# Gating each expert's result as it is stored, and summing the stored rows and the residual ahead of the last products

## The chip, the cores and the metric

The kernel runs on one core of one Trainium2 chip. The metric is the device time of one execution in microseconds; times are given as the median of several runs. TensorE is called PE here, its weight loads PEld, VectorE DVE, ScalarE ACT, GpSimd POOL, and SyncE, which issues most of the DMAs, SP.

## The reference

The program is a trunk of two layers over 256 context rows and 256 latent rows of width 1024. Each layer first mixes tokens and then runs a mixture of 32 experts, of which every row uses two. The change lies in the first layer's mixture, where all 512 rows take part. Cut to what matters:

```
h_c = layer_norm(xc) * (1 + cscale2) + cshift2
h_l = layer_norm(x)  * (1 + scale2)  + shift2
ffn = moe(concat([h_c, h_l]))          # each row: sum over its 2 experts of
                                       #   w[row, e] * swiglu(row; gate[e], up[e]) @ down[e]
xc = post_norm(ALPHA * xc + cgate2 * ffn[:256])
x  = post_norm(ALPHA * x  + gate2  * ffn[256:])
```

The gate is one row of 1024 numbers for all context rows (`cgate2`) and another for all latent rows (`gate2`). These are the two classes of tokens. `post_norm` is a layer norm with a scale and an offset.

## The kernel before

The 512 rows lie in four tiles of 128: tiles 0 and 1 are context, tiles 2 and 3 latent. An expert takes up to 64 rows. For each expert of the first mixture `expert0` (L1769) gathers its rows from DRAM with an indirect DMA on POOL, multiplies them with the gate and up weights (`product`, L1722, four loads of 1 MB), makes the activation `th` on ACT and DVE (`swiglu`, L1692), and multiplies with the down weights (`down`, L1733, two loads of 1 MB). Row `p` of the result has the first half of the columns of a slot in partitions 0 to 63 and the second half in 64 to 127. ACT copies it out of PSUM times the slot's weight `w` (L1787), and POOL scatters it to `yb_d` in DRAM with a second indirect DMA: rows 0 to 511 are the rows' first experts, rows 512 to 1023 their second. Two spare slots (32 and 33) take the 65th row and later ones of busy experts, at most 64 each; what goes beyond is left to the overflow loop.

The results of experts 30 and 31 aren't scattered. They are kept as a rounded part `yh` and the rest `yl` (L1784, L1785), and selection products with `slt` (L1933) add them to the tiles. This is what the title calls the last products.

After expert 29 SP loads, for tiles 0 and 1, both stored rows and the residual, and for tiles 2 and 3 the first stored row (L1912 to L1922). The two stored rows of tiles 0 and 1 are summed (L1917), and for each tile DVE adds the last products (L1937). Then comes `overflow` (L1512), a loop whose count is read from memory and is zero here; all engines meet at it. Behind it, for each tile: the gate product, for tiles 2 and 3 the second stored row, and the residual (L1948 to L1960), on DVE and POOL, and then `normed_affine` (L1961), which takes statistics on DVE, a power on POOL and two further steps on DVE. The next layer starts with a second norm over the same tiles (`h_in`, L471), whose result `xh` PE transposes.

Buffers are tiles of stacked pools; a tile waits until whoever used its place is done. The order on each queue is laid out when the program is built, by a list scheduler that follows a model of time and takes what is ready by priority; `tc.high_priority` and `tc.issue_after` bend it. Each engine then works through its queue in order. SP's queue too is in order: a load that waits for its buffer holds all behind it.

The second mixture (`experts1`, L1845) is not touched by the change, apart from the shared overflow code, where it keeps what it does.

## Time and profile before

| what | us |
|---|---|
| median of 3 runs | 2546.49 (2543.59 to 2548.29) |
| the profiled execution | 2547.03 |
| its span, first to last instruction | 2545.2 |
| PE busy | 2204.2 (87%) |
| DVE busy | 1396.3 (55%) |
| ACT busy | 693.5 (27%) |
| POOL busy | 719.0 (28%) |
| bytes moved by DMA | 710.71 MB, mean 279 GB/s |

The busy shares are means over stages with different limits. What the change is worth has to be read from its own stage: the slices show where a stage begins, the windows which engine fills it, the waits who holds whom up, and the timeline in what order. The chain that ended last is cut at the second mixture's overflow loop and reaches back only 14 us, so it says nothing on the first mixture.

### The profile page before, as it was taken

The page shows a single profiled execution, that of the slowest core. Times are in us where ns is not written, and L with a number is a line of the kernel's source. Part 1 is how long each engine was busy: PE and PEld are TensorE (multiplying, and loading weights), DVE is VectorE, ACT ScalarE, POOL GpSimd, SP SyncE. Part 2 cuts the span into 40 slices and gives each one's busy share as a digit, 9 for nine tenths or more (in the row PEclk, how much of TensorE's full clock was granted, in tenths as well). Part 3 has the DMA queues.
Part 4 walks back from the last instruction along what each step waited for, and adds up shares of the span by engine and source line. Part 5 has one row for each costly group of instructions (what it writes and reads, how often), then busy time and mean ns, then how long its engine had stood idle before and what let it go on. Part 6 is the DMA issues. An engine that isn't in the chain of part 4 may idle for free. (4 is left out here: it accounts for less than half of the span.)

```text
span 2545.2 us, 41555 instructions
## 1 busy us (share of the span) xinstructions
PE 2204.2 (87%) x16198; PEld 1523.7 (60%) x16198; DVE 1396.3 (55%) x2787; ACT 693.5 (27%) x1344; POOL 719.0 (28%) x686
## 2 busy tenths in 40 slices
PE   5898997799999979878888829998789879999996
PEld 3687865577565755444444427797677645555553
DVE  7947789957676742000000086366788665545444
ACT  2334421244564111111111113352366211111110
POOL 8988877862210131111111030101143010000000
PEclk8999998899999979999999959999899879999998
DMA  6644476678767679999999958649664699999996
GB/s 250 180 139 123 136 210 188 183 230 271 233 179 229 232 293 351 414 405 414 404 409 411 374 206 223 217 134 272 192 208 131 208 366 372 421 422 421 423 421 269
DMA packets 326999, 710.71 MB, mean 279 GB/s; under 512 B 40654, under 2 KB 240766, under 8 KB 274064
## 3 DMA queue, kind: packets, MB, share of 16 engines
q1 hardware_dynamic: 320080, 694.72, 76.4%
q0 software_dynamic: 5280, 8.05, 1.0%
q10 hardware_dynamic: 1440, 5.24, 0.5%
q8 instruction: 130, 2.13, 0.3%
q14 instruction: 69, 0.57, 0.1%
HBM read 645.82 MB, written 71.37 MB: 282 GB/s over the span
## 5 line engine op out<-in xcount | busy, mean ns | idle before, releaser
L1729 PE MATMUL pgu<-mraw,xgt 128*64 128x256 f32 x4224 | 496.6, 387 | 28.3 <-DMA mraw<-in_moe_w_up_dram 25.7
L1729 PEld LDWEIGHTS pgu<-mraw,xgt 128*64 128x64 f32 x4224 | 298.2, 139 | 221.6 <-DMA mraw<-in_moe_w_up_dram 57.1
L84 DVE SCALAR_TENSOR_TENSOR th<-th,pgu 128x256 f32<-128x256 f32 x132 | 55.5, 421 | 499.9 <-ACT th L1694 497.7
L1749 PE MATMUL pd<-mraw,at 128*64 128x512 f32 x1056 | 253.2, 608 | 43.6 <-DMA mraw<-in_moe_w_down_dram 41.7
L525 PE MATMUL pfm<-hhi,lo 128*128 128x256 f32 (+1 forms) x832 | 283.5, 344 | 7.8 <-DVE lo L78 7.2
L523 PE MATMUL pfm<-hhi,hi 128*128 128x256 f32 (+1 forms) x832 | 284.9, 346 | 4.9 <-ACT hi L93 4.3
L524 PE MATMUL pfm<-hlo,hi 128*128 128x256 f32 (+1 forms) x832 | 285.4, 344 | 2.1 <-DVE hlo L78 2.1
L78 DVE TENSOR_TENSOR lo<-raw,hi 128x1024 fp32r<-128x1024 f32 (+1 forms) x147 | 205.3, 1398 | 84.4 <-ACT hi L93 82.3
L93 ACT ACTIVATE hi<-raw 128x1024 fp32r<-128x1024 f32 (+1 forms) x160 | 169.3, 1059 | 188.2 <-PE pfm L524 115.1
L128 POOL TENSOR_TENSOR bnrs<-bnrs,mhalf 128x1 f32<-128x1 f32 x26 | 28.7, 1110 | 643.0 <-DVE bnrs L88 642.9
L1749 PEld LDWEIGHTS pd<-mraw,at 128*64 128x64 f32 x1056 | 71.2, 137 | 188.2 <-issue 113.5
L525 PEld LDWEIGHTS pfm<-hhi,lo 128*128 128x128 f32 x832 | 158.9, 192 | 31.5 <-DVE lo L78 8.8
L523 PEld LDWEIGHTS pfm<-hhi,hi 128*128 128x128 f32 x832 | 159.4, 193 | 29.3 <-issue 7.0
L524 PEld LDWEIGHTS pfm<-hlo,hi 128*128 128x128 f32 x832 | 159.7, 192 | 23.6 <-issue 5.2
L78 DVE TENSOR_TENSOR acc<-acc,po 128x512 f32<-128x512 f32 x124 | 79.6, 682 | 99.8 <-PE po L1837 99.7
L1789 POOL DMA_INDIRECT yb_d<-ye,idx x30 | 30.0, 999 | 297.3 <-ACT ye L93 297.0
L523 PE MATMUL pm<-yh,hi 128*128 128x512 f32 (+1 forms) x256 | 88.1, 360 | 11.3 <-DVE gatel L84 7.0
L524 PE MATMUL pm<-yl,hi 128*128 128x512 f32 (+1 forms) x256 | 90.1, 354 | 5.3 <-DVE yl L78 5.3
L523 PE MATMUL ptm<-hi,hhi 128*128 128x256 f32 x320 | 92.7, 291 | 0.0
L524 PE MATMUL ptm<-lo,hhi 128*128 128x256 f32 x320 | 92.0, 288 | 0.0
L84 DVE SCALAR_TENSOR_TENSOR yg<-pd,wcol,g 64x512 f32<-64x512 f32 x64 | 48.0, 749 | 79.7 <-PE pd L1749 79.2
L525 PE MATMUL ptm<-hi,hlo 128*128 128x256 f32 x320 | 91.6, 287 | 0.0
(506 smaller groups left out, 4359.6 us busy)
## 6 DMA issues: line engine op xcount, KB each, us to landing
mraw<-in_moe_w_gate_dram SPq DMA_DIRECT2D x132, 1024.0 KB
mraw<-in_moe_w_up_dram SPq DMA_DIRECT2D x132, 1024.0 KB
mraw<-in_moe_w_down_dram SPq DMA_DIRECT2D x132, 1024.0 KB
raw<-in_w_in_dram SPq DMA_DIRECT2D x116, 512.0 KB
modr<-in_mod_w_dram SPq DMA_DIRECT2D x80, 512.0 KB
modw<-in_mod_w_dram SPq DMA_DIRECT2D x8, 1024.0 KB
gt_d<-gt SPq DMA_DIRECT2D x16, 512.0 KB
q_d<-Q SPq DMA_DIRECT2D x32, 256.0 KB
```

The source lines that it names most:

```text
L78: V.tensor_tensor(o, a, b, op=op)
L84: V.scalar_tensor_tensor(o, a, s, b, op0=op0, op1=op1)
L93: S.activation(o, a, AF.Copy, scale=scale)
L128: G.tensor_tensor(o, a, b, op=OP.pow)
L523: T.matmul(p, ahi, bhi, start=first, stop=False)
L524: T.matmul(p, ahi, blo, start=False, stop=False)
L525: T.matmul(p, alo, bhi, start=False, stop=last)
L1729: o = T.matmul(p[64 * cb:64 * cb + 64, 256 * i:256 * i + 256], xt[:, kt], raw[:, k, 256 * cb:256 * cb + 256], start=(kt == 0), stop=(kt == ...
L1749: o = T.matmul(p[64 * nh:64 * nh + 64], at[:, j, 64 * cb:64 * cb + 64], raws[cb][:, j, nh], start=(k == 0), stop=(k == 3))
L1789: sc_ = G.indirect_dma_start(out=yb_d.rearrange("r (n c) -> (r n) c", n=2), out_offset=bass.IndirectOffsetOnAxis(ap=i, axis=0), in_=y, in_ ...
```

## The change

Each expert's result is multiplied by the gate of its slot's class before it is stored. A tile `g2n` holds both classes' gate rows in the split form of the result, and `cls` holds, for each slot of each expert, whether its row is of the one class or the other (token number under 256 or not). Three DVE instructions (a scaling by one class column, a product and sum with the other, and the product with the result and the weight) stand in place of ACT's copy. For experts 30 and 31 the product goes to a tile first, and `yh` and `yl` are made from that. In the overflow loop the gate is applied likewise. All four tiles now load both stored rows and the residual before the last products, through two buffers each for the second row and the residual; the rows are summed on DVE (tile 3: POOL) and the residual added on DVE. What stood behind the overflow loop for this goes, with its two gate rows. `craw`, used at the program's start, moves from the constants to a pool of its own that is closed afterwards.

```diff
--- before.py
+++ after.py
@@ -136,8 +136,8 @@
 
     x_d = [A["xin"], dram.tile([512, D], F32, name="x1_d")]
     cond = const.tile([128, KT, 32], F32, name="cond")
-    craw = const.tile([128, 2, KT, 2], F32, name="craw")
-    with tc.high_priority():
+    with tc.tile_pool(name="crp", bufs=1) as wk, tc.high_priority():
+        craw = wk.tile([128, 2, KT, 2], F32, name="craw")
         dma(craw[:, 0], A["cond"])
         S.activation(craw[:, 1], craw[:, 0], AF.Tanh, scale=0.5)
         stt(craw[:, 1], craw[:, 1], 1.0, craw[:, 0], OP.add, OP.mult)
@@ -1345,7 +1345,7 @@
         if l == 0:
             rt.update(oh=[new([128, 4, 32], f"oh{k}") for k in range(2)], wgt=new([128, 3, 4], "wgt"),
                       pos=new([128, 2, 4], "pos"), idx=new([128, 2, 32], "idx", I32), tok=new([128, 2], "tok"), wsl=new([128, 32], "wsl"),
-                      sidx=new([128, 2, 2], "sidx", I32), swsl=new([128, 2], "swsl"),
+                      sidx=new([128, 2, 2], "sidx", I32), swsl=new([128, 2], "swsl"), cls=new([128, 2, 34], "cls"),
                       pidx=pb("pidx")[:, :96])
         else:
 
@@ -1446,6 +1446,8 @@
             V.tensor_copy(rt["idx"], val)
             V.tensor_copy(rt["wsl"], rt["pidx"][:, 64:96])
             V.tensor_copy(rt["tok"], val[:, 0, 30:32])
+            ts(rt["cls"][:, 0, :32], val[:, 0], 256.0, None, OP.is_lt)
+            ts(rt["cls"][:, 1, :32], val[:, 0], 256.0, None, OP.is_ge)
 
     def route_over(rt, wk):
 
@@ -1507,6 +1509,8 @@
             stt(val, pi[:, 0:2], -1.0, emp, OP.add, OP.add)
             ts(val[:, 1:2], val[:, 1:2], 2.0, second, OP.mult, OP.add)
             V.tensor_copy(rt["sidx"][:, :, b], val)
+            ts(rt["cls"][:, 0, 32 + b:33 + b], val[:, 0:1], 256.0, None, OP.is_lt)
+            ts(rt["cls"][:, 1, 32 + b:33 + b], val[:, 0:1], 256.0, None, OP.is_ge)
             V.tensor_copy(rt["swsl"][:, b:b + 1], pi[:, 2:3])
 
     def overflow(rt, acc, g2):
@@ -1613,6 +1617,9 @@
                     for k in range(4):
                         T.matmul(p[:rows], at_[:, k], raw[:, k], start=(k == 0), stop=(k == 3))
                     copyS(y[:rows, 512 * nh:512 * nh + 512], p[:rows], scale=wcol[:rows])
+                gg = g2
+                if l == 0:
+                    gg = [mod_bc(wk, l, 5, c, f"og{c}") for c in range(2)]
                 slt = wk.tile([128, nt, 128], F32, name="oslt")
                 if l == 0:
                     for t in range(nt):
@@ -1628,11 +1635,9 @@
                         po = pc("opo")
                         cs = slice(512 * nh, 512 * nh + 512)
                         T.matmul(po, slt[:rows, t], y[:rows, cs], start=True, stop=True)
-                        if l == 1:
-                            yg = wk.tile([128, 512], F32, tag="oyg", name="oyg")
-                            tt(yg, po, g2[1][:, cs], OP.mult)
-                            po = yg
-                        tt(acc[t][:, cs], acc[t][:, cs], po, OP.add)
+                        yg = wk.tile([128, 512], F32, tag="oyg", name="oyg")
+                        tt(yg, po, gg[t // 2 if l == 0 else 1][:, cs], OP.mult)
+                        tt(acc[t][:, cs], acc[t][:, cs], yg, OP.add)
 
     def moe(rt, keep):
         l, nt = rt["l"], rt["nt"]
@@ -1664,6 +1669,11 @@
             xg = [fx.tile([128, D], F32, name=f"xg{i}") for i in range(2)]
             for i in range(2):
                 G.memset(xg[i], 0.0)
+            g2n = fx.tile([128, 2, 512], F32, name="g2n")
+            for c in range(2):
+                for nh in range(2):
+                    m = mods[0, 10 + nh, c, :]
+                    dma(g2n[64 * nh:64 * nh + 64, c], bass.AP(tensor=m.tensor, offset=m.offset, ap=[[0, 64], [1, 512]]))
         else:
             acc = [fx.tile([128, D], F32, name=f"acc{t}") for t in range(nt)]
 
@@ -1767,7 +1777,7 @@
             return xt, p
 
         def expert0(e, xt, pgu, nxt):
-            y = wk.tile([128, 512], F32, tag="y", name="ye", bufs=3) if e not in (30, 31) else None
+            y = wk.tile([128, 512], F32, tag="y", name="ye", bufs=3)
             front = nxt()
             product(pgu, 1, e, xt)
             a = swiglu(pgu[:, :256], pgu[:, 256:], 256)
@@ -1779,12 +1789,16 @@
             p = pc("pd")
             down(p, e, a)
             w = rt["wsl"][:, e:e + 1] if e < 32 else rt["swsl"][:, e - 32:e - 31]
+
+            gr = wk.tile([128, 512], F32, tag="gr", name="gr", bufs=1)
+            ts(gr, g2n[:, 0], rt["cls"][:, 0, e:e + 1])
+            stt(gr, g2n[:, 1], rt["cls"][:, 1, e:e + 1], gr, OP.mult, OP.add)
+            stt(y, p, w, gr, OP.mult, OP.mult)
             if e in (30, 31):
                 yh, yl = y2[e - 30]
-                copyS(yh, p, scale=w)
-                stt(yl, p, w, yh, OP.mult, OP.subtract)
+                copyS(yh, y)
+                tt(yl, y, yh, OP.subtract)
                 return front
-            copyS(y, p, scale=w)
             i = rt["idx"][:, 1, e:e + 1] if e < 32 else rt["sidx"][:, 1, e - 32:e - 31]
             sc_ = G.indirect_dma_start(out=yb_d.rearrange("r (n c) -> (r n) c", n=2),
                                        out_offset=bass.IndirectOffsetOnAxis(ap=i, axis=0),
@@ -1909,17 +1923,14 @@
             expert0(31, *f, lambda: None)
         with tc.issue_after(rt["load"].ins):
             if l == 0:
-                xs = [bc.tile([128, D], F32, name=f"fx{t}") for t in range(2)]
-                for t in range(2):
-                    y1 = lp_.tile([128, D], F32, tag="y1", name="y1", bufs=2)
+
+                for t in range(nt):
+                    y1, x1 = [lp_.tile([128, D], F32, tag=n, name=n, bufs=2) for n in ("y1", "x1")]
                     for i, y in enumerate((acc[t], y1)):
                         dma(y, yb_d[ntok * i + 128 * t:ntok * i + 128 * t + 128, :])
-                    tt(acc[t], acc[t], y1, OP.add)
-                for t in range(2):
-                    dma(xs[t], x1_d[128 * t:128 * t + 128, :])
-                for t in range(2, nt):
-                    dma(acc[t], yb_d[128 * t:128 * t + 128, :])
-                g2 = {0: mod_bc(bc, l, 5, 0, "g20")}
+                    dma(x1, x1_d[128 * t:128 * t + 128, :])
+                    (tg if t == 3 else tt)(acc[t], acc[t], y1, OP.add)
+                    stt(acc[t], x1, ALPHA, acc[t], OP.mult, OP.add)
             lg = bc_row(bc, part_bcast(A["ln2_g"][l], 128), "lg2")
             lb = bc_row(bc, part_bcast(A["ln2_b"][l], 128), "lb2")
         if l == 0:
@@ -1939,25 +1950,10 @@
         pwk.close()
         overflow(rt, acc, g2)
         fp = keep.enter_context(tc.tile_pool(name=f"fin{l}", bufs=2, side="right", reuse_waits="tile"))
-        if l == 0:
-            g2[1] = mod_bc(fp, l, 5, 1, "g21")
 
         for t in range(nt):
             rows = slice(128 * t, 128 * t + 128)
             x = acc[t]
-            if l == 0:
-                f = tg if t else tt
-                if t < 2:
-                    f(x, x, g2[0], OP.mult)
-                    stt(x, xs[t], ALPHA, x, OP.mult, OP.add)
-                else:
-                    y = fp.tile([128, D], F32, tag="y", name="y")
-                    dma(y, yb_d[ntok + 128 * t:ntok + 128 * t + 128, :])
-                    f(x, x, y, OP.add)
-                    f(x, x, g2[1], OP.mult)
-                    xt = fp.tile([128, D], F32, tag="x", name="fx")
-                    dma(xt, x1_d[128 * t:128 * t + 128, :])
-                    stt(x, xt, ALPHA, x, OP.mult, OP.add)
             normed_affine(fp, x, x, lg, lb)
             dma(x_d[1][rows, :] if l == 0 else out[0, rows, :], x)
         ph.close()
```

## Rows read from the trace of the kernel before

**Rows 1.** The page's 40 slices, PE and DMA, busy tenths.

```profile
PE   5898997799999979878888829998789879999996
...
DMA  6644476678767679999999958649664699999996
```

**Rows 2.** Windows: length, busy PE PEld DVE ACT POOL; PEclk, DMA, GB/s.

```profile
940.00:950.00 10.00, 10.00 (x78) 5.82 (x76) 1.68 (x4) 0.93 (x3) 0.00 (x0) 1.00 1.01 426
...
985.00:1443.00 458.00, 380.79 (x2633) 202.37 (x2631) 27.96 (x77) 59.66 (x117) 55.09 (x56) 0.98 1.01 404
...
1465.00:1482.90 17.90, 5.79 (x19) 3.62 (x17) 11.14 (x14) 2.23 (x3) 0.04 (x1) 0.57 0.89 333
...
1482.90:1515.00 32.10, 0.03 (x1) 0.03 (x1) 31.77 (x45) 1.32 (x2) 21.75 (x11) 0.50 0.27 99
...
1515.00:1530.00 15.00, 14.51 (x100) 12.53 (x100) 13.92 (x33) 7.62 (x10) 1.06 (x2) 0.76 0.85 271
```

**Rows 3.** Waits from 1440 to 1545: us in total, times, longest.

```profile
ACT xh L242 <- DVE bnnb L84: 47.4, 2, 45.9
...
PE pht L479 <- ACT xh L242: 38.6, 2, 38.3
...
PE po L1933 <- DVE fa L78: 5.9, 1, 5.9
```

**Rows 4.** DVE's groups, 1482.8 to 1513.6: busy us, mean ns | idle before.

```profile
L84 DVE SCALAR_TENSOR_TENSOR fa<-fx,fa 128x1024 f32<-128x1024 f32 x4 | 8.9, 2254 | 0.0
...
L84 DVE SCALAR_TENSOR_TENSOR fa<-fa,bnmv,lg 128x1024 f32<-128x1024 f32 x4 | 5.1, 1274 | 0.0
...
L84 DVE SCALAR_TENSOR_TENSOR fa<-fa,bnrs,lb 128x1024 f32<-128x1024 f32 x3 | 4.5, 1516 | 0.0
...
L78 DVE TENSOR_TENSOR fa<-fa,g 128x1024 f32<-128x1024 f32 x1 | 3.4, 3383 | 5.5 <-DMA y<-yb_d 5.5
```

**Rows 5.** POOL's groups from 1462 to 1532, the same view.

```profile
L81 POOL TENSOR_TENSOR fa<-fa,g 128x1024 f32<-128x1024 f32 x3 | 8.5, 2834 | 36.0 <-DMA y<-yb_d 36.0
...
L81 POOL TENSOR_TENSOR fa<-fa,y 128x1024 f32<-128x1024 f32 x2 | 6.6, 3322 | 0.0
```

**Rows 6.** Timeline 1462 to 1477, SP and DVE: start us, us, instruction [idle].

```profile
1462.40 0.55 SPq L1916 DMA_DIRECT2D y<-yb_d  x1
...
1466.41 3.94 SPq L513 DMA_DIRECT2D raw<-in_w_in_dram  x3
...
1469.33 1.23 DVE L78 TENSOR_TENSOR fa<-fa,y 128x1024 f32<-128x1024 f32 x1 [0.30 <-DMA y<-yb_d]
...
1476.08 1.29 DVE L78 TENSOR_TENSOR fa<-fa,po 128x512 f32<-128x512 f32 x2 [0.37 <-PE po L1933]
...
1476.67 0.34 SPq L1955 DMA_DIRECT2D y<-yb_d  x1
```

**Rows 7.** Windows of 1 us around the end of the loads.

```profile
1479.00:1480.00 1.00, 0.00 (x0) 0.00 (x0) 0.00 (x0) 0.00 (x0) 0.00 (x0) 0.50 1.00 385
...
1480.00:1481.00 1.00, 0.00 (x0) 0.00 (x0) 0.00 (x0) 0.00 (x0) 0.00 (x0) 0.50 0.09 29
```

**Rows 8.** DVE's timeline at the loop of the second mixture.

```profile
2530.30 1.29 DVE L78 TENSOR_TENSOR acc<-acc,po 128x512 f32<-128x512 f32 x2 [0.70 <-PE po L1837]
...
2533.31 0.69 DVE L225 BATCH_NORM_STATS2 bnst<-acc 128x6 f32<-128x512 f32 x1 [1.71 <-issue]
```

**Rows 9.** Timeline of the first two experts.

```profile
948.09 0.88 DVE L84 SCALAR_TENSOR_TENSOR th<-th,pgu 128x256 f32<-128x256 f32 x2 [7.02 <-ACT th L1694]
...
948.19 3.65 PE L1749 MATMUL pd<-mraw,at 128*64 128x512 f32 x16
...
951.89 0.69 ACT L93 ACTIVATE ye<-pd,wsl 128x512 f32<-128x512 f32 x1 [3.83 <-PE pd L1749]
```

**Rows 10.** DVE's timeline: a scaling from SBUF, a product from PSUM.

```profile
1541.34 0.55 DVE L90 TENSOR_SCALAR cvy<-xp,convw 128x512 f32<-128x512 f32 x1 [3.62 <-DMA convw<-in_conv_dram]
...
1463.32 0.75 DVE L84 SCALAR_TENSOR_TENSOR yl<-pd,wsl,yh 128x512 fp32r<-128x512 f32 x1 [5.57 <-ACT yh L93]
```

## What the change should do to the time

> **What bounds the kernel now.** I read the page's slices first. TensorE (PE) is busy in nine slices of ten, and where it is not, the DMA engines are: in slices 17 to 23 (the experts of the first mixture) PE falls to 7 or 8 and DMA stays at 9. In slice 24 PE drops to 2 [rows 1]. Then I cut the span by stage. From 985 to 1443 us DMA is at its full share and moves 404 GB/s while PE works 381 of 458 us and VectorE (DVE) 28: this stage is bound by its weights [rows 2]. From 1482.9 to 1515.0 PE does nothing at all, DMA moves 99 GB/s, and DVE is busy for 31.8 of 32.1 us: here one engine holds everything up, and it is DVE [rows 2]. The waits of that stretch say the same: PE waits 38.3 us for the normalised rows `xh`, ScalarE, which makes them, waits 45.9 us for DVE's `bnnb` [rows 3]. After 1515 PE is busy again for 14.5 of 15 us [rows 2], so an earlier start of the second layer is worth its whole length as long as its operands keep up. So the change is judged by three stretches: the experts (up to 1465), the sums ahead of the overflow loop (1465 to 1483), the work behind it (1483 to 1515).
>
> **Behind the loop: what goes.** DVE's groups from 1482.8 to 1513.6 [rows 4] hold the gate product of tile 0, 3.4 us, and four residual sums `fa<-fx,fa`, 8.9 us. Both leave. The three `lb` steps took 1.52 us each where the same shape with `lg` takes 1.27, which is 0.8 us in all; two of them ran while GpSimd (POOL) worked beside them. POOL's five additions and products, 8.5 + 6.6 us [rows 5], leave this stretch too, so I count those 0.8 us as saved. Sum: 3.4 + 8.9 + 0.8 = 13.1 us. Left are 30.8 - 13.1 = 17.7 us of DVE work between the loop and the first `xh`, if the order stays. Of the rest, two `lg` steps and one `lb` step belong to tiles 2 and 3 (2 x 1.27 + 1.2 = 3.7 us) and need not stand ahead of tile 0. The list scheduler fills waits with them now; I leave them, and keep 14.0 us as the lower end.
>
> **Ahead of the loop: what comes.** New on DVE are the sum of tile 2's two stored rows, 1.23 us like that of tile 0 [rows 6], and four residual sums at 1.27 us, 6.3 us in all. DVE has next to no room there: 11.1 of 17.9 us busy [rows 2], and 5.5 of the idle time is the wait at the loop itself [rows 4]. By DVE's work alone the last addition of a product, which now ends at 1476.08 + 1.29 = 1477.4, ends at 1483.7.
>
> The loads may be later than that. `y1` and `x1` have two buffers each, so tile 2's second row waits for tile 0's sum (1469.33 + 1.23 = 1470.6) and its residual for the next step (1471.8); tile 3's wait for tile 1's, behind two additions of a product (1474.4 and 1475.7). These four loads stand in SP's queue among the first weights of the next layer, which SP issues up to 1470.35 [rows 6] and which need the same DMA engines; behind them nothing of this stretch is queued. Now the DMA engines are full until 1480, and in the microsecond after that they move 29 GB/s [rows 7]. Out go one gate row and one `y` load, 1.05 MB; in come 2.1 MB. The difference at some 385 GB/s (estimate from the stretch around it) is 2.7 us, so the last load lands near 1482.7. The residual sum (1.27) and the additions (1.29) then end at 1485.3. Tile 3's first sum runs on POOL, where such a sum took 2.3 to 3.3 us; its row lands 1.4 us before the last load, so this path gives 1481.3 + 3.3 + 1.27 + 1.29 = 1487.2. I take 1486. Upper end: each late load takes the 6.9 us that `y` took from 1462.4 to 1469.3 [rows 6], which gives the same 1487.2, and one DVE step beside POOL costs 3.4 instead of 1.2 us (2.1 more): 1489.4.
>
> One rule of the Trainium skill bears on this POOL sum. The trace shows a DVE product at 3.38 us beside POOL [rows 4] where a sum of that shape took 1.23 alone [rows 6]. The Trainium skill, SBUF — State Buffer, "Who interferes with whom", says that a DVE instruction with two SBUF inputs and a GpSimd instruction that reads SBUF exclude each other for a whole instruction. The trace agrees in kind. By that rule DVE would lose POOL's whole 2.3 us wherever it has work then, and the sum below would be 6.0 instead of 8.3 us; I expect DVE to be waiting for tile 3 at that time and take nothing.
>
> **The loop itself.** From the last addition to the first work behind it 5.5 us pass now, put down to a `y` load [rows 4] that SP issued at 1476.67, just ahead of the loop [rows 6]; the DMA engines run dry at 1480 [rows 7]. In the second mixture, with no load under way, the same loop costs 1.7 us: the last addition ends at 2531.59, the statistics start at 2533.31 [rows 8]. After the change every load of the stretch has been used before the loop, so I take 1.7; the upper end is 5.5. The loop's body grows, but no instruction of it ran, so its new gate rows cost nothing.
>
> **The sum.** The loop is left at 1486 + 1.7 = 1487.7 instead of 1482.9, 4.8 us later (ends: 1483.7 + 1.7, 2.5 us; 1489.4 + 5.5, 12.0 us). Behind it 13.1 us are gone. Net 8.3 us less (10.6 to 1.1, and 14.3 with the better order). The first `xh` starts near 1505.4 instead of 1513.7.
>
> **The experts.** Each of 34 experts gives up one ScalarE copy of 0.69 us [rows 9] and gets three DVE steps of 128 x 512: a scaling (0.55), a sum of two products, and the product out of PSUM (0.75 as for `yl`) [rows 10], so 2.05 us if both of the latter take 0.75. DVE has 430 idle us of 458 there [rows 2], the first two steps depend on nothing of the expert, and the store is used only at the end: nothing on the path. If that cover were gone it would be 34 x 2 = 70 us. For the last expert the chain becomes product, copy, difference, where it was copy, difference: 0.7 us more. It is hidden by PE's wait of 5.9 us for tile 0's sum [rows 3], and costs 0.7 without it. The new gate tile is 0.5 MB in four SP issues at the stage's start. At 404 GB/s it would cost 1.3 us within the weight-bound stretch; I take 0, since it is asked for before that stretch, with 1.3 as the upper end. The moved `craw`, the class columns (four kinds of small DVE steps at some 0.2 us) and the new places of tiles I take at 0, with half a microsecond either way.
>
> The profiled execution took 2547.0 us (span 2545.2 and 1.8 around it); the median of the runs is 2546.5. The sum against the first gives 2538.7, carried to the median 2538.2. I say 2538.5.
>
> **Rivals.**
> First, the late loads eat it: the two-buffer loads come at their upper end and the loop still finds a load under way. For it: DMA is full there already. Against it: only 1 MB more is moved. Net 1.1 to 4 us: 2542.5 to 2545.5.
>
> Second, it goes better: tiles 0 and 1 go through the normalisation first and PE starts on 14.0 us instead of 17.7. For it: all four sums are there when the loop ends. Against it: PE then needs tiles 2 and 3 soon after, and DVE's work on them is the same. Net 8.3 + 3.7 = 12.0 us, up to 14.3: 2532 to 2534.5.
>
> Third, slower: the result of an expert now stands in DVE's own queue, which is in order. Now `th` of the next expert runs at 948.09 while this one's last products run from 948.19 to 951.8 and ScalarE copies it out at 951.89 [rows 9]. If the result is queued ahead of that `th`, it waits 3.8 us and then takes 0.75, and PE, which is busy without a gap there [rows 2], stands still for 4.55 us per expert. It decides from two experts on (9.1 against 8.3 us). With five experts before 985 it is 22.8 - 8.3 = 14.5 us slower: 2561. Against it: PE's and DVE's orders come from one time model, which now sees `th` first. Later, at 985 to 1443, PE idles 77 us, 2.6 per expert, and would hide most of it.
>
> **How the numbers follow.** Forecast 0.55, spread over 2534.5 to 2543; eaten 0.20; better 0.16; slower 0.09. A measurement of this kernel tells about 0.2%, 5.1 us, from no change: under 2541.4 is faster. That takes nine tenths of the forecast and the better case, 0.65; within it lie a tenth of the forecast, the eaten case and little else, 0.26; slower 0.09. The range 2531 to 2549 holds forecast, better and eaten with their bounds, the 1.3 us of the gate tile, and leaves out most of the slower case and the edges.
>
> **What would show it.** Behind the loop no gate product, no `fa<-fx,fa` and no POOL sum; the first `xh` some 18 us after the loop (14 in the better case); the last addition near 1486 and the loop's wait near 1.7 us. If the wait stays at 5.5 us or the last addition comes after 1489, the first rival holds. DVE's busy time from 985 to 1443 rises from 28 to some 90 us with the stage's length unchanged within 1.3 us; if PE waits there for DVE's `th`, the third holds. I am wrong in kind if PE, after an earlier start, stands still for tiles 2 and 3.

## The result: 15.5 us slower, for the most part where the change computes nothing

| | us |
|---|---|
| before, median of 4 runs | 2546.39 (2543.59 to 2548.29) |
| after, median of 4 runs | 2561.92 (2560.32 to 2564.36) |
| ratio | 1.0053, interval 1.0038 to 1.0068 |
| span of the profiled execution, before and after | 2545.2 and 2558.4 |

The forecast was 2538.5, in a range of 2531 to 2549. In the stretch that the forecast was about, the profile after shows the change doing what it was said to do. These are windows of the kernel after (length; busy PE, PEld, DVE, ACT, POOL; granted clock, DMA share, GB/s); they answer to [rows 2].

```profile
985.00:1443.00 458.00, 377.68 (x2621) 199.87 (x2618) 85.15 (x165) 39.03 (x86) 59.59 (x57) 0.99 1.01 401
...
1499.00:1519.20 20.20, 0.00 (x0) 0.00 (x0) 20.14 (x42) 0.00 (x0) 6.56 (x6) 0.50 0.26 104
1519.20:1534.00 14.80, 13.23 (x96) 11.43 (x97) 11.84 (x30) 8.98 (x11) 1.10 (x2) 0.78 0.61 209
```

From the overflow loop to the first `xh` DVE now works for 20.2 us, where it was 30.8 before. Its groups on DVE (busy us, mean ns; idle before) answer to [rows 4]: gate product and residual sums are gone, and the idle time of 5.5 us at the loop has become 1.7.

```profile
L225 DVE BATCH_NORM_STATS2 bnst<-fa 128x6 f32<-128x512 f32 x8 | 5.4, 679 | 1.7 <-issue 1.7
L226 DVE BATCH_NORM_STATS2 bnst<-fa 128x6 f32<-128x512 f32 x8 | 5.4, 678 | 0.0
L84 DVE SCALAR_TENSOR_TENSOR fa<-fa,bnmv,lg 128x1024 f32<-128x1024 f32 x4 | 5.1, 1277 | 0.0
L84 DVE SCALAR_TENSOR_TENSOR fa<-fa,bnrs,lb 128x1024 f32<-128x1024 f32 x4 | 4.9, 1268 | 0.0
```

PE's wait for the first `xh` shows the same from the other side (total, times, longest); it was 38.6 us in [rows 3].

```profile
PE pht L479 <- ACT xh L242: 32.5, 2, 32.2
```

Ahead of the loop the late loads of tiles 2 and 3 show in the timeline of SP and DVE (start, length, instruction, idle time before it), which answers to [rows 6]:

```profile
1480.50 1.27 SPq L1930 DMA_DIRECT2D y<-yb_d  x1
...
1489.46 1.23 DVE L78 TENSOR_TENSOR fa<-fa,y 128x1024 f32<-128x1024 f32 x1 [3.28 <-DMA y<-yb_d]
...
1496.06 1.28 DVE L78 TENSOR_TENSOR fa<-fa,po 128x512 f32<-128x512 f32 x2
1499.06 0.69 DVE L225 BATCH_NORM_STATS2 bnst<-fa 128x6 f32<-128x512 f32 x1 [1.72 <-issue]
```

Then I cut both executions into five stretches at instructions that both have: the routing's last conversion (`idx`), the last `yh` of the experts, the first `xh` of the second layer, the last router product (`plg`) there, and the end. Lengths in us, worked out from the trace to some 0.1 us; the last four kernels are described below.

```
                     to idx  experts  to xh  mixer 2  mixture 2    span
before                924.2    538.4   51.1    536.0      495.5  2545.2
before, once more     923.2    533.8   51.8    537.6      493.3  2539.7
after                 930.3    542.6   46.3    541.2      498.0  2558.4
before_pad32          930.0    542.1   51.1    544.7      497.6  2565.5
expert_pad            921.9    541.1   51.0    536.8      495.7  2546.5
after_mended_early    923.5    534.8   45.9    537.0      494.0  2535.2
inplace_right         926.0    529.7   46.3    532.2      489.4  2523.6
```

The third column is the whole of the forecast, and it is 4.8 us shorter. All the other columns are longer in the kernel after: 6.1, 4.2, 5.2 and 2.5 us. The first of these ends before any gate or sum of the change has run (only the four loads of `g2n` have, at 901 us), and the last two begin after all of them. Two profiles of the one kernel before differ by up to 4.6 us in a column, so a single column proves little; that all four grow was the question.

### The profile page after: what moved, and what is told of

Its sections match the earlier page's. It is cut to its first block, busy times and chain, and to the rows that moved or that the text cites. A ratio compares the mean times of both kernels' runs of the same rounds, so it can differ in the third digit from the quotient of the medians.

```text
span 2558.4 us, 41632 instructions
## 1 busy us (share of the span) xinstructions
PE 2213.4 (87%) x16198; PEld 1534.9 (60%) x16198; DVE 1453.1 (57%) x2895; ACT 671.4 (26%) x1312; POOL 706.3 (28%) x682
## 3 DMA queue, kind: packets, MB, share of 16 engines
q10 hardware_dynamic: 1440, 5.24, 0.5%
## 5 line engine op out<-in xcount | busy, mean ns | idle before, releaser
L84 DVE SCALAR_TENSOR_TENSOR ye<-pd,wsl,gr 128x512 f32<-128x512 f32 x32 | 24.0, 751 | 260.8 <-PE pd L1759 260.8
L1704 ACT ACTIVATE th<-pgu 128x256 f32<-128x256 f32 x66 | 25.4, 385 | 484.2 <-PE pgu L1739 484.2
L81 POOL TENSOR_TENSOR P<-P,smx 128x512 f32<-128x512 f32 (+1 forms) x48 | 44.6, 951 | 179.0 <-DVE smx L1069 107.3
```

The lines of the kernel that those rows point to most:

```text
L81: G.tensor_tensor(o, a, b, op=op)
L84: V.scalar_tensor_tensor(o, a, s, b, op0=op0, op1=op1)
L1704: S.activation(th, pg, AF.Tanh, scale=0.5)
```

## Experiments

Three theories. A: the moved `craw` is loaded late, and what hangs on it is laid out later and in another order. B: the experts' new steps and the sums cost the time. C, formed after the first runs and called P in later expectations: the tiles lie on other places, and that alone costs it. Where an expectation says E, it means the opposite of P: the work, the waits or the order cost it. Ratios are to the kernel before, on the same chip.

**One part at a time.** `craw_alone` makes only the first hunk of the diff in the kernel before:

```diff
-    craw = const.tile([128, 2, KT, 2], F32, name="craw")
-    with tc.high_priority():
+    with tc.tile_pool(name="crp", bufs=1) as wk, tc.high_priority():
+        craw = wk.tile([128, 2, KT, 2], F32, name="craw")
```

> The kernel before with one edit of the change alone: craw moves from the constants to a small pool of its own, and nothing else. In the changed kernel the load of craw stands at 17.3 us instead of 2.6 us, and the first products of the modulation wait 11.6 us for cond. Theory A (the start): the pool takes the place that the raw identity matrix held, so the load waits until that matrix is copied, and the whole first mixer is laid out later and in another order. Then the row numbers of the gather (idx) are ready near 930 us instead of 924.2 and the run takes 2551 to 2556 us. Theory B (the experts and what lies behind them cost the time): idx stays within 1 us of 924 and the run within 2 us of the kernel before, 2546.4.

Measured: 2560.89 (ratio 1.0078, 1.0059 to 1.0097), more than either theory gave. Two lines that change nothing in what is computed cost as much as the whole change. The timelines of both kernels show what they do at once. Before, and then after:

```profile
2.59 0.43 SPq L141 DMA_DIRECT2D craw<-in_cond_dram  x1
```

```profile
17.27 0.36 SPq L141 DMA_DIRECT2D craw<-in_cond_dram  x1
```

The new pool takes the place of the pool of `identw`, which has just been closed, so the load can't go ahead of the copy of the identity matrix, which ends at 11.8 us in the kernel after, and it then stands in SP's queue behind other loads. PE waits 11.2 us for it. Not all of that is lost, since for the weights of the same product PE waits 22.2 us in the first 60 us before and 3.8 after. PE's wait (waits of the kernel after; total, times, longest):

```profile
PE pm L164 <- DVE cond L88: 11.2, 1, 11.2
```

`craw_beside` is the kernel after with `craw` allocated in that earlier pool, next to `identw`, so that its load starts at 2.6 us again:

```diff
     with tc.tile_pool(name="idp", bufs=1) as wk:
         raw = wk.tile([128, 128], F32, name="identw")
         ...
+        craw = wk.tile([128, 2, KT, 2], F32, name="craw")
```

> The changed kernel whole, but craw is placed beside the raw identity matrix in the same short-lived pool, so that its load waits for nothing. Theory A: the load is back near 2.6 us, idx back near 924 us, and 6 us or more of the 15.5 are gone: 2550 to 2556 us; if the start also set the order of all later stages, more is gone, and the run lands at 2538 to 2547. Theory B: less than 2 us are gone, 2560 to 2562.

Measured: 2559.72 (1.0065, 1.0048 to 1.0082). The load is early again and nothing is won, close to what B gave. Theory A is not enough.

`one_col` is the kernel after with `craw` back in the constants. To make room it has one class column instead of two, and one step instead of two for the gate row:

```diff
+            tt(g2n[:, 0], g2n[:, 0], g2n[:, 1], OP.subtract)
...
-            ts(gr, g2n[:, 0], rt["cls"][:, 0, e:e + 1])
-            stt(gr, g2n[:, 1], rt["cls"][:, 1, e:e + 1], gr, OP.mult, OP.add)
+            stt(gr, g2n[:, 0], rt["cls"][:, e:e + 1], g2n[:, 1], OP.mult, OP.add)
```

`gate_old_tail` is the same with the tail of the kernel before, without its gate products: the gates alone, and no sums moved ahead.

> The changed kernel with craw left among the constants as before, and room made for it by one class column instead of two: the gate is the latent gate plus a class column times the difference of the two gates, one DVE instruction per expert less. The instructions of the first layer's mixer stand in the same order as in the kernel before. Theory A: idx within 1 us of 924.2; what the rest of the change does is then seen bare. By the terms of the prediction (last addition 1486, loop 1.7, 17.7 us behind it) 2538.5; by what the changed kernel showed from its gather to its first xh (0.6 us less than before) and no loss later, about 2546; Theory B: 2554 or more.

> As one_col, but the stored rows and the residual are summed as in the kernel before: tiles 0 and 1 sum their rows ahead of the loop, everything else stands behind it, only without the gate products. It tells the gating from the early sums. If the early sums bring what was forecast, this kernel is slower than one_col by some 5 us (behind the loop 5 to 9 us of DVE work and the loop's wait of 5.5 us stay, ahead of it 6 us less). If the late loads eat it, it is as fast as one_col or faster.

Measured: 2553.34 (1.0045, 1.0028 to 1.0062) and 2547.44 (1.0020, 1.0005 to 1.0035). Their stretches to `xh` are 46.9 and 45.9 us: the gates alone give the gain of that stretch, and the sums moved ahead add nothing to it. By the medians the kernel without them is even 5.9 us faster, where the first case expected it some 5 slower; the two profiles differ by 1.2 the other way. But `one_col` has the order of the kernel before in the whole first mixer, and its `idx` still comes 6.5 us late, where theory A had it within 1 us. Theory B can't explain that either, though the time is close to its 2554: nothing of the experts has run by then.

**The same order, other places.** `before_again` is the kernel before, profiled once more. `before_beside` is the kernel before with the edit of `craw_beside`. `one_col_bufs` is `one_col` with more places for the late loads:

```diff
-y1, x1 = [lp_.tile([128, D], F32, tag=n, name=n, bufs=2) for n in ("y1", "x1")]
+y1, x1 = [lp_.tile([128, D], F32, tag=n, name=n, bufs=k) for n, k in (("y1", 4), ("x1", 3))]
```

> The kernel before once more, unchanged, for a second profile on the chip of the experiments. One column with `craw` kept has the instruction order of the kernel before up to the routing, and its profile still runs 3.8 us late from 400 us on and 6.5 us late at `idx`. If that is how far two profiles of one kernel differ, this profile drifts by 3 to 6 us against the first one too, and nothing before 924 us in that kernel was lost. If the class columns and tiles placed by the change cost it (theory B), this one stays within 1 us of the first, `idx` at 923.5 to 925.2.

> The kernel before with `craw` taken out of the lasting pool and put beside the identity matrix's tile in the pool at the program's start, so that its place is given back as in the change but its load waits for nothing. Theory A (what costs in the change is that the load of `craw` waits until 17 us for the place of the identity matrix, and that all that follows is then laid out in another order): the order stays that of the kernel before but for a few lines, and the time is that of the kernel before, 2543 to 2549. Theory C (any new place for the tiles costs several us, whatever the start): 2553 to 2561, as with `craw` alone moved.

> One class column, `craw` kept, and four places for the second stored rows (three for the residual rows) instead of two each, so that no load of tiles 2 and 3 waits for the sums of tiles 0 and 1. If the late loads set the end of the sums (tile 2's row lands 8.9 us after its issue, DVE idle 3.3 us for it), the last addition comes 4 to 7 us earlier against the end of the experts and the kernel takes 2546 to 2550 where the one with two places took 2553.3. If the gain is eaten behind (layer 1 laid out in another order, or DVE's work behind the loop), the last addition comes earlier but the time stays at 2552 to 2556.

Measured: a span of 2539.7 for `before_again`, with `idx` at 923.2, so this profile has no drift like that of `one_col`; 2561.56 (1.0055, 1.0038 to 1.0072) for `before_beside`; 2560.97 (1.0053, 1.0037 to 1.0070) for `one_col_bufs`, above both of its cases. The middle one decides. All engines but SP, which has one load moved at the start, have their orders unchanged, the load of `craw` is early, and still 14 us are lost. What differs is that all tiles laid out behind `craw` lie 128 bytes lower, by the places that the pools hand out. In `one_col` and in the change they lie 160 bytes higher.

`one_col_bufs` shows the price of the late loads: its stretch to `xh` is 44.4 us, 2.5 less than in `one_col`. It loses more than that in the second mixer, 546.7 against 532.7 us, which comes out in another order there.

**Only the places.** `before_pad32` adds to the kernel before a tile that nothing uses. `beside_pad` puts the same tile into `before_beside`, so that all places are as before. `inplace` is `one_col` with the class column in `craw`'s own tile, which is free by then, and the two last columns in spare room of `swsl`, so that nothing else moves; `inplace_bufs` has the more places of `one_col_bufs` besides.

```diff
     craw = const.tile([128, 2, KT, 2], F32, name="craw")
+    padc = const.tile([128, 32], F32, name="padc")
```

```diff
-swsl=new([128, 2], "swsl"), cls=new([128, 34], "cls"),
+swsl=new([128, 4], "swsl"), cls=craw.rearrange("p a b c -> p (a b c)"),
```

> The kernel before with one tile more in the lasting pool, 128 bytes in each partition, that nothing writes or reads. Every engine's order of instructions stays as it was; only the places of the tiles that are laid behind it (of the mixers, the experts' buffers on the left side, the gates) move up by 128 bytes. Theory P (the places of the tiles set the time: those behind `craw` lie 160 bytes higher in the change and 128 lower with `craw` moved): 2552 to 2562, though nothing is computed or loaded otherwise. Theory E (the change's own work and its waits cost the time; the slower kernel with `craw` put beside the identity matrix owes it to its start 2 us later): 2543 to 2550 as before.

> The kernel before with `craw` beside the identity matrix's tile, which took 2561.6 with all later tiles 128 bytes lower, and an unused tile of 128 bytes where `craw` was, so that all later tiles lie where they lay. Theory P: 2543 to 2550, the time of the kernel before. Theory E (the start's new order of loads costs it): stays at 2556 to 2562.

> One class column (2553.3 with tiles 160 bytes higher) with the column written into `craw`'s own tile once that is used up and the two columns of the second expert group into spare room, so that every lasting tile and all the mixers' tiles lie where the kernel before has them; the order of instructions is that of the one-column kernel. Theory P: the layers' mixers lose nothing (drift at `idx` within 2 us of a profile of before), and what is left is the tail's own gain against the late loads: 2540 to 2546. Theory E: 2551 to 2556 as the one-column kernel.

> The same with four places for the second stored rows and three for the residual rows, which took the last addition 3.7 us earlier but had the second layer laid out on other places. Theory P leaves open where these tiles come to lie in the second layer; if the places there agree, 2537 to 2543, the forecast of the change less its placement. If it stays over 2550, the second layer's places or order still cost.

Measured: 2556.82 (1.0048, 1.0028 to 1.0067); 2544.63 (0.9993, 0.9982 to 1.0005); 2534.64 (0.9956, 0.9938 to 0.9974); 2546.19 (1.0000, 0.9988 to 1.0011). 128 bytes that nobody reads or writes cost 11.7 us, and 128 bytes in the old place take the 14 us of `before_beside` back. With its places kept, the one-column kernel turns from 0.45% slower to 0.44% faster, 5 us under the range expected. `one_col_bufs` and `inplace_bufs` have one order too, and go from 1.0053 to 1.0000. In all profiles with an early load of `craw`, `idx` comes at 921.9 to 926.9 us where the mixers' tiles have their old places or lie 256 or 768 bytes from them (`u_pad` below moves one stage only), and at 929.1 to 935.3 where they lie 128 or 160 off. `inplace_bufs` missed its forecast: its stretch to `xh` is the shortest of all, 43.9 us, but its second mixer takes 545.5 us where `inplace` takes 529.8. Its order differs there, and `one_col_bufs`, of the same order on other places, takes as long (546.7); what in that order costs is open.

**The change itself, with its places mended.** `after_mended` is the change with the conditioning table packed (its product's other rows are not used) and an unused tile that brings all later tiles to the places of before; every engine's order is that of the change but for one small step. `after_mended_early` also has `craw` back in the constants. `craw_alone_pad` is `craw_alone` with an unused tile of 128 bytes in the old place. `before_m256` is the kernel before with all later tiles 256 bytes lower.

```diff
-    cond = const.tile([128, KT, 32], F32, name="cond")
+    cond, padc = const.tile([128, 48], F32, name="cond"), const.tile([128, 168], F32, name="padc")
...
-cond[:, kt, :]
+cond[:, 2 * kt:2 * kt + 32]
```

> The change as it stands, each engine's order of instructions as in it, with every tile of the mixers, experts and gates back at the place that the kernel before gives it: the table of 8 x 32 conditioning columns is packed into 48 columns (the rows of its product that change are not used), and an unused tile fills up the rest. Theory P (the places cost 11 to 16 us, the change itself gains): 2540 to 2549, which is 13 to 20 us less than the change; 256-byte packets near 29 ns instead of 40. Theory A (the late load of `craw` costs several us in the start and in what is laid out after it): 2550 to 2556, since that load still waits.

> The same, and `craw` back in the lasting pool, so that its load starts at 2.6 us as before; two class columns as in the change; all later tiles at the places of before. Theory P: near the one-column kernel with kept places (2534.6), 2533 to 2541, since what is left between them is one DVE step of 0.5 us per expert beside the weights. If the second column's step or its load costs something, 2541 to 2546.

> The kernel before with all tiles behind the conditioning table moved 256 bytes down (packed table and an unused tile), same order of instructions but for one small step. 128 up and 128 down both cost 12 to 16 us. If what counts is the place against a step of 256 bytes, this takes 2543 to 2550 as before, 256-byte packets near 29 ns. If it is a step of 512 bytes or the places themselves (which tile neighbours which), 2553 to 2562.

> `craw` alone moved to a pool of its own (2560.9), with an unused tile of 128 bytes in its old place, so that nothing else moves; order of instructions as in that kernel. Theory P: 2544 to 2551, the late load (17.3 instead of 2.6 us) costs 0 to 5 us. Theory A: 2553 to 2561.

Measured: 2548.40 (1.0006, 0.9996 to 1.0016); 2542.31 (0.9984, 0.9975 to 0.9994); 2544.17 (0.9992, 0.9979 to 1.0006); 2550.55 (1.0018, 1.0007 to 1.0030). Three fell in the range of their first case; `after_mended_early` fell in its second, 2541 to 2546. So the change is taken apart. By the ratios, with 2546 us for 1: the change 13.5 us slower; places mended 1.5 slower; load early too, 4.1 faster. The places cost 12.0 us, the late load 5.6 (each give or take some 4, from the intervals), and what the change was made for gains 4.1. `craw_alone_pad` finds 4.6 for the late load without the rest of the change. Both prices hold the load together with the order that the queues get by it, which differs in hundreds of places; no run parts the two. And 256 bytes down cost nothing where 128 down cost 14.0: what counts is the place against a step of 256 bytes.

**Through which loads.** In the kernel before, the tiles on the left side that are loaded most (`raw`, `U`, the left-hand weight buffers) begin on multiples of 256 bytes. `u_pad` moves the stage of `U` off it, which is loaded in rows of 256 bytes; `expert_pad` moves the left-hand buffers and tiles of the experts.

```diff
-            U = s1.tile([128, 32, 64], F32, name="U")
+            padu, U = s1.tile([128, 32], F32, name="padu"), s1.tile([128, 32, 64], F32, name="U")
```

```diff
+        padm = ph.enter_context(tc.tile_pool(name=f"mpad{l}", bufs=1)).tile([128, 32], F32, name="padm")
         left = ring(ph, 5, "left")
```

> The kernel before with 128 unused bytes ahead of the tile `U` of each layer's state-space stage, which is loaded in rows of 256 bytes; that stage's tiles move up by 128 bytes, all others stay. Order of instructions as before. The profiles of kernels with moved tiles lose 3 to 5 us at 320 to 400 us and 2 to 3 at 1700 to 1760, where these rows are loaded at 47 to 56 ns a packet instead of 24 to 36. If the load of `U` is what the places cost in the mixers: 2550 to 2555, packets near 48 ns. If it is other tiles of the mixers or the experts: 2543 to 2549.

> The kernel before with 128 unused bytes ahead of the left-hand weight buffers of both layers' experts; those buffers and the tiles of the expert stages move up by 128 bytes, the mixers' tiles stay. Order of instructions as before. Profiles of kernels with moved tiles drift by 4 to 7 us between 1000 and 1440 us and by 4 to 6 between 2360 and 2520, those with kept places by 0 to 4 and 0 to 3. If the places cost in the experts too: 2549 to 2556. If all of it is in the mixers: 2543 to 2548.

Measured: 2548.93 (1.0025, 1.0013 to 1.0037) and 2552.40 (1.0041, 1.0026 to 1.0056). Both intervals exclude no effect, and the two losses, 5.3 and 8.8 us against the runs of before beside them, make up the 11.7 of `before_pad32` within their intervals. `expert_pad` came as expected. `u_pad` missed: its time lies in the range of the other case, its loss under the 6 to 11 expected, and its 256-byte packets took 38 to 39 ns, not 48: in `before_pad32` the other loads of that stage are moved as well, and there the packets take 49. That load, in windows of `before_again` and then of `before_pad32` (the last two columns are DMA share and GB/s): the DMA engines are as busy in both, and move a quarter less in the second.

```profile
346.00:348.00 2.00, 2.00 (x10) 1.65 (x9) 1.28 (x4) 0.44 (x1) 1.77 (x5) 1.00 1.38 134
348.00:350.00 2.00, 2.00 (x10) 1.61 (x10) 1.97 (x3) 1.10 (x2) 1.84 (x4) 1.00 1.39 135
```

```profile
350.00:352.00 2.00, 2.00 (x10) 1.63 (x9) 1.02 (x3) 0.33 (x2) 1.78 (x4) 1.00 1.44 107
352.00:354.00 2.00, 2.00 (x11) 1.61 (x10) 1.97 (x4) 1.39 (x2) 1.82 (x4) 1.00 1.43 96
```

By the trace's packet records a 256-byte packet of this load takes 34 ns (mean) in the first and 49 in the second, and PE then waits for `U` 3.6 us in `before_pad32`, 2.0 in `u_pad` and not at all in the two profiles of before. For the experts a window of 400 us that is bound by weights, of the kernels before, `before_pad32`, `expert_pad` and `after_mended` in turn; the last number is GB/s:

```profile
1040.00:1440.00 400.00, 324.25 (x2222) 169.22 (x2218) 22.23 (x60) 49.82 (x97) 46.25 (x47) 0.97 1.01 410
```

```profile
1040.00:1440.00 400.00, 321.01 (x2232) 168.03 (x2228) 23.06 (x62) 50.94 (x99) 48.21 (x49) 0.99 1.02 406
```

```profile
1040.00:1440.00 400.00, 321.99 (x2202) 167.76 (x2200) 22.23 (x60) 49.82 (x97) 46.25 (x47) 0.98 1.01 407
```

```profile
1040.00:1440.00 400.00, 326.15 (x2259) 170.95 (x2255) 72.70 (x137) 33.76 (x74) 51.23 (x49) 0.99 1.01 412
```

The change itself moves 407 there and its mended form 412. The weights' packets of 8192 bytes take 309 ns (median) with kept places and 313 with moved ones. The engines' own steps don't get longer: from the kernel before to `before_pad32` the durations of ACT's instructions, 761 us in all, change by 0.4 us, and those of DVE's, 1543 us, by -4.3.

**The other way round.** The right-hand tiles, among them those of 212 of the experts' 396 weight loads, lie 224 bytes past a multiple of 256 even in the kernel before. If the cause is right, putting them on it must gain. `inplace_right` adds 224 unused bytes at that end to `inplace`, and packs the conditioning table for the room, the left-hand tiles moving by three whole steps.

```diff
+    padr = ctx.enter_context(tc.tile_pool(name="rpad", bufs=1, side="right")).tile([128, 56], F32, name="padr")
```

> The one-column kernel with kept places (2534.6), and 224 unused bytes at the far end of the memory, so that the right-hand tiles (212 of the experts' 396 weight buffers, the modulation weights, the sums' tiles), which lie 224 bytes past a step of 256 in the kernel before, come to lie on a step too; the left-hand tiles move down by 768 bytes, three whole steps, with the conditioning table packed to make the room. Order of instructions the same but for some ten at the start. If what costs is a start off the step of 256 bytes, the experts' weight-bound stretches speed up: moving the left-hand buffers off the step cost 8.8 us, so putting the right-hand ones on it gives 5 to 9 us: 2525 to 2530. If only the step between tiles loaded in 256-byte rows and their places counts, or the stretches are bound elsewhere: 2532 to 2537.

Measured: 2525.62 (0.9922, 0.9898 to 0.9947), as expected: 20 us faster than the kernel before and 9 faster than `inplace` (give or take 8, from the intervals). The window of `inplace_right` that answers to the four above:

```profile
1040.00:1440.00 400.00, 333.71 (x2330) 177.73 (x2327) 62.90 (x116) 35.09 (x77) 59.14 (x50) 0.98 1.01 414
```

Experts and second mixture, 536.6 and 493.1 us in `inplace`, take 529.7 and 489.4. The packets of 8192 bytes in this window show the cause directly: 309 ns or less is what 62% of them take in the kernel before, where the left-hand tiles alone lie on the step, 61% in `inplace`, 21% in `before_pad32` and 22% in `expert_pad`, where neither side does, and 92% in `inplace_right`, where both do.

## Why the prediction was wrong, step by step

**The step that failed** is the last sentence on the experts: "The moved `craw`, the class columns [...] and the new places of tiles I take at 0, with half a microsecond either way." The new places cost 12.0 us, and the moved `craw`, its late load with the order that follows from it, 5.6 (by the ratios of the mended kernels). Both ends of that term were guessed; no row stood behind it. For `craw` the diff itself would have shown the wait: a pool opened where one was just closed, and PE's first products behind the load. For the places there was no such row in the trace of before, but there was a number to check: by how many bytes the tiles behind it move.

The Trainium skill, DMA: Bandwidth & Descriptors, "How a descriptor splits into AXI transactions", has the rule that I did not weigh: a descriptor is cut into pieces of 256 bytes at multiples of 256, so one whose length is a multiple of 256 and whose start is not takes a piece more, and the bytes ahead of its start still cost beats of 32 bytes. The Trainium skill tells this of reading; here it is the place written to that moved. The runs agree in kind: 128 and 160 bytes cost, 256 does not. An estimate by the beats that the Trainium skill counts there: 128 bytes off a multiple a row of 256 bytes takes 12 for 8, half more, and the trace has 49 ns for 34; one of 8192 takes 260 for 256, 1.6% more, and the trace has 313 for 309, 1.3%.

**Behind the loop, 17.7 us forecast, 20.1 measured.** The gate product, the residual sums and POOL's work are gone, as the forecast had it. But in the profile of before only seven pairs of statistics (below, the same view as [rows 4]) and three `lb` steps stood ahead of the first `xh`; now eight and four do (groups above). That is 1.2 and 1.2 us of a later tile's work that moved ahead, all of the miss.

```profile
L226 DVE BATCH_NORM_STATS2 bnst<-fa 128x6 f32<-128x512 f32 x7 | 4.7, 672 | 0.0
L225 DVE BATCH_NORM_STATS2 bnst<-fa 128x6 f32<-128x512 f32 x7 | 4.7, 668 | 0.0
```

The better order of the second rival did not come; the order went the other way.

**Ahead of the loop, 1486 forecast.** The last addition ends at 1497.3, 24.4 us after the last `yh` begins; the forecast had 23.4 (1486 less 1462.6). The late loads were to take 6.9 us each at the upper end; `y` of tile 2 was issued at 1480.50 and used at 1489.46, 9.0 us later. With more buffers the stretch to `xh` was 2.5 us shorter in both pairs of kernels (46.9 to 44.4, 46.4 to 43.9), so the first rival took 2.5 us but not the whole.

**The loop, 1.7 us forecast, 1.72 measured.** This term was right, and its reason fits: the loads of the stretch had been used.

**The rule on POOL's sum** would have cost DVE 2.3 us. POOL's sum ran from 1492.08 for 2.35 us, and DVE's two additions of a product, started at 1492.07, took 1.29 us as they do alone. These read one operand from PSUM, so the rule, which is about two operands from SBUF, was not put to the test. Its price did not come: behind them DVE had nothing to do but wait 1.37 us for its next step, which needs the sum (timeline of the kernel after).

```profile
1492.07 1.29 DVE L78 TENSOR_TENSOR fa<-fa,po 128x512 f32<-128x512 f32 x2
1492.08 2.35 POOL L81 TENSOR_TENSOR fa<-fa,y 128x1024 f32<-128x1024 f32 x1 [35.48 <-DVE fa L84]
1494.73 1.23 DVE L84 SCALAR_TENSOR_TENSOR fa<-x,fa 128x1024 f32<-128x1024 f32 x1 [1.37 <-SPq L1524]
```

**The sum.** Net 8.3 us were forecast for this stretch and 5.2 came: 50.9 to 51.8 us in four profiles with the old sums and kept places, 45.9 to 46.3 in the change and both mended forms. The stretch got shorter, as forecast, but by 3 us less. Which part gave the gain was not as I had it: `gate_old_tail` has the same 45.9 without any sum moved ahead, so taking the gate products out gives it alone, and no run shows a gain from the early sums. The 4.1 us by which `after_mended_early` beats the kernel before fit this gain, with an interval of 1.5 to 6.4.

**The experts, 0 forecast.** With kept places they take 534.8 and 535.2 us in the two mended forms, and 533.8 to 538.4 in four profiles without the new steps: nothing to be seen, as forecast. The third rival, the result ahead of the next `th`, would have shown in PE's wait for `th`. That is 9.6 us before and 9.3 after (PE's groups in the kernel before and then after, 985 to 1443 us; idle time and who ended it).

```profile
L1738 PE MATMUL pat<-identr,th 128*128 128x128 f32 x58 | 14.1, 325 | 10.0 <-DVE th L84 9.6 <-DVE off L88 0.4
L1748 PE MATMUL pat<-identr,th 128*128 128x128 f32 x56 | 13.4, 321 | 9.7 <-DVE th L84 9.3 <-DVE off L88 0.4
```

The kernel came out at the 2561 of that rival, but by another mechanism: the number agreeing proves nothing.

**What stays open.** `inplace` beats `after_mended_early` by 7.7 us (medians; 7.1 by the ratios) although it saves only one hidden step per expert; in the profiles 7.2 us lie in the second mixer (529.8 against 537.0 us), whose order differs. Kernels of one order differ there by 6 us from profile to profile (531.7 to 537.6), so part of it may be scatter. Why the orders of the second mixer take 530 to 546 us was not tested, nor the gates without the early sums on kept places.

## What to carry to other kernels

When an edit adds, drops or moves a tile that lives long, count by how many bytes all tiles behind it move, and keep them on multiples of 256 with padding; to test a suspicion, add an unused tile and change nothing else. A pool opened right behind a closed one makes its first load wait for the old one's last reader, so look at who reads that place, and at what PE does with the load. Before an edit is judged, compare it with a form of itself whose places and first loads are those of the kernel before: here that turned a loss of 13.5 us into a gain of 4.1.

## What the hardware showed that I had not expected

128 unused bytes ahead of the working tiles cost 11.7 us of 2545 (before_pad32), and 224 at the other end helped `inplace` by 9. It is the loads: in the weight-bound window DMA moved 406 to 407 GB/s with the left-hand buffers off a multiple of 256 bytes, 409 to 412 with them on it, and 414 with both sides on it. Two profiles of the one kernel before, at spans of 2545.2 and 2539.7, differ by 4.6 us in the experts' stretch alone; a drift of that size in one profile is not a finding.
